# Wide predicated copies in a chunked linear recurrence, and a shorter weight look-ahead ahead of paired blocks

## The chip, the cores and the metric

The kernel runs on one core of a Trainium2 chip. Its engines each work through an instruction stream of their own: TensorE (PE) multiplies matrices, with weight loads (PEld) that overlap the products; VectorE (DVE), ScalarE (ACT) and GpSimd (POOL) compute elementwise; SyncE (SP) issues most transfers. The metric is the device time of one execution in microseconds (us). Before the change it is 2135.25 us, the median of three runs (2132.23 to 2136.88).

## The reference, cut to what matters

Two layers (DEPTH 2) work on 512 frames of width 1024, in float32. Each layer has a half-step SwiGLU feed-forward block (inner width 2816), a token mixer, a cross-attention into 256 memory tokens and a second feed-forward block:

```python
def swiglu(h, w1, w3, w2):
    return (jax.nn.silu(h @ w1) * (h @ w3)) @ w2

# mixer, head group A: 4 heads, key and value width 128
S_t = diag(f_t) S_{t-1} + k_t outer v_t      # k_t = 1 - f_t
o_t = S_t^T q_t
# head group B: trailing means over 2, 4, 8, 16 frames minus the frame, then a linear map
x = x + concat(o_a, o_b) @ w_out
```

The causal score of frame t against an earlier frame s inside a chunk is the sum over the key width of q_t, k_s and the product of all decays f between them. This part, and the feed-forward products, are what the change touches.

## The kernel before, in words

**Layout.** Activations lie with features on the 128 partitions and the 512 frames along the free axis. Each float32 operand is split into a high and a low part of the type that TensorE multiplies fast (`split`: a CAST on ACT, line 76, writes the high part `whi`, a subtraction on DVE, line 77, writes the low part `wlo`), and every product is three matmuls (`mm3`, lines 84 to 86: high by high, high by low, low by high). So nearly all of the time is in lines 84 to 86.

**Order of the work.** The program text sets an order, and a scheduler that simulates the engines places the instructions of each engine's stream; in a stream, everything runs in that fixed order, and an instruction that waits holds all behind it. Rings of tiles limit how far work runs ahead: one shared ring ("s") of 38 SBUF tiles holds weights as loaded (`raw`, `wsum`), weights split (`whi`, `wlo`), and mixer tiles such as `spread` and `packed`. A transfer into a ring tile waits until the tile's last reader is done.

**Weights.** `Weights` is a list of all weight pieces in order of use. A piece is a column tile (1024 by 128), a group of rows, or a *block*: two neighbouring column tiles of which a Strassen-like scheme (`Pairs`) forms sums. A block is loaded by four transfers on SP's queue (lines 130 to 133) and a fifth on POOL's queue that adds the second column tile onto the first in memory (line 134); it is then split in several steps (raw, the loaded sum, sums made on DVE in lines 163 and 164, and a quarter tile `w`). `next` is called when a piece is to be used: it finishes the splits under way, and then starts the splits of the pieces ahead. `ahead(i, n)` walks on from piece i until n units are passed, a block counting two. The split look-ahead is 4 units where the piece itself is a block and `SPLIT` = 5 elsewhere; the load look-ahead is `LOAD` = 7. The feed-forward blocks use plain column tiles for the first 6 or 8 of 22 column tiles, then blocks, in three parts, each followed by its rows of w2. So the list passes from plain pieces to blocks 11 times in the program.

In `Pairs.block` a product's result stays in PSUM until ACT has copied it (`keep`, line 545) or DVE has added it; between products, `wts.step()` takes the next split step. `xall` (line 436) adds the finished rows of w2 to the residual on DVE.

**The mixer's levels.** Scores inside a chunk of 128 frames are built by doubling: at level m = 1, 2, 4, ... 64, frames pair up in runs of 2m, the second half of a run against the first half. `atd` holds the scores of two heads (one *pair of heads* g) over four chunks. For m from 2 to 16, `dense` lets TensorE multiply the packed first halves (`keys`) with the second halves of `qf` (line 768), ACT copies the PSUM result to `packed` (line 777), and transfers on ACT's queue (line 782) spread its rows over the partitions where they belong, into the tile `spread`, which was set to zero once. `place` then copies, under a mask, from `spread` into `atd` (line 740; for m = 1 straight from PSUM): one copy of 128 partitions by 64 elements per head and chunk. At m = 32, `dense` copies small tiles from PSUM (line 773); at m = 64 TensorE multiplies directly (line 815) and DVE copies (line 816). After each level, `kg` and `qf` are multiplied by the decay of the run (`tot`; lines 822 and 824, one operation per head) and `tot` by itself (line 827). The copies of level m/2 stand in the program behind the first pair's decays of level m.

`levels` is a generator that is stepped between other work of the mixer: the value projection (`v`, line 906), the pooling head group (`u` line 917, POOL's additions into `sa` and `sb` line 920, `pt` lines 924 to 926), and weight splits. Behind the levels, `states` transposes `kg` (line 847, copied to `kt` by ACT) and multiplies it with `v` (line 856).

Of the kernel before, what the change touches and what calls it, by code (L numbers as in the profile page):

```python
# [7 lines left out]
F32 = mybir.dt.float32  # L8
# [3 lines left out]
ALU = mybir.AluOpType  # L12
AX = mybir.AxisListType

P = 128
D = 1024
T = 512
# [3 lines left out]
NT = T // P  # L21
# [25 lines left out]
def trunk_kernel(ctx: ExitStack, tc: tile.TileContext, ap: dict, out: bass.AP):  # L47
    nc = tc.nc
    pe, act, dve, pool = nc.tensor, nc.scalar, nc.vector, nc.gpsimd
# [11 lines left out]
    def ps_tile():  # L61
        return pp.tile([P, 512], F32, tag="ps", name="ps")
# [5 lines left out]
    def s_tile(shape, dt, name):  # L68
        return sp.tile(shape, dt, tag="s", name=name)
# [19 lines left out]
    class Weights:  # L89
# [107 lines left out]
        def next(self):  # L197
            i = self.at
            self.at += 1
            while self.todo:  # L200
                self.step()
            block = len(self.src[i]) == 2
            ahead = [*self.ahead(i, 4 if block else self.SPLIT)]
            if i + 3 == len(self.src) - 1:
                ahead.append(i + 3)
            for j in ahead:
                if j not in self.hl:
                    self.todo.append(self.cut(j))
                    if not block or j == i:
                        while self.todo:  # L210
                            self.step()
            for j in self.ahead(i, self.LOAD):
                self.load(j)
            return self.hl.pop(i)
# [53 lines left out]
    masks = {}  # L268
# [421 lines left out]
    def mix(l, norm, mem, after):  # L690
        f = [s_tile([P, 2, T], F32, "f") for _ in range(2)]
        kg = [s_tile([P, 2, T], F32, "kg") for _ in range(2)]
        q = [s_tile([P, 2, T], F32, "q") for _ in range(2)]
        qf = [s_tile([P, 2, T], F32, "qf") for _ in range(2)]
        atd = [s_tile([P, 2, NT, P], F32, "atd") for _ in range(2)]
# [24 lines left out]
        def products(a, b):  # L720

            t = tp.tile([P, T], F32, tag="sq", name="qk", bufs=4)
            hl = s_tile([P, 2, T], F32R, "qkp")
            pool.tensor_tensor(t if len(a.shape) == 2 else t.rearrange("p (h n) -> p h n", h=2), a, b, op=ALU.mult)
            split(hl[:, 0], hl[:, 1], t)
            return hl

        def column_sums(ps, hl):

            for c in range(2):  # L730
                pe.matmul(ps, ones_r, hl[:, c], start=c == 0, stop=c == 1)

        def place(g, m, rows):

            for hh in range(2):
                o = atd[g][:, hh].rearrange("p i (b e j) -> p i b e j", e=2, j=m)
                src = rows[:, hh * 256:(hh + 1) * 256].rearrange("p (i b j) -> p i b j", i=NT, j=m)
                mk = masks[m].rearrange("p (b j) -> p b j", j=m)
                for i in range(NT):
                    dve.copy_predicated(o[:, i, :, 1, :], mk, src[:, i])  # L740

        keys = [None, None]

        def first_halves(g, m):


            keys[g] = tp.tile([P, T], F32, tag="sq", name="keys", bufs=4)
            src = kg[g].rearrange("p h (b e j) -> p h b e j", e=2, j=m)[:, :, :, 0, :]
            if m > 4:
                act.copy(keys[g].rearrange("p (h b j) -> p h b j", h=2, j=m), src)  # L750
                return
            for hh in range(2):
                dst = keys[g][:, hh * HT:(hh + 1) * HT].rearrange("p (i j b) -> p i b j", i=NT, j=m)
                act.copy(dst, src[:, hh].rearrange("p (i b) j -> p i b j", i=NT))

        spread = s_tile([P, 2, T], F32, "spread")
        pool.memset(spread, 0.0)
        packed = [None]

        def dense(g, m):  # L760


            ps = ps_tile()
            for hh in range(2):
                for i in range(NT):
                    c = hh * HT + i * 64
                    b = qf[g][:, hh, i * P:(i + 1) * P].rearrange("p (b e j) -> p b e j", e=2, j=m)[:, :, 1, :]
                    pe.matmul(ps[0:64, c:c + 64], keys[g][:, c:c + 64], b, start=True, stop=True)
            if m == 32:
                for b in range(2):  # L770
                    src = ps[b * 32:b * 32 + 32].rearrange("p (h i t) -> p h i t", h=2, i=NT)[:, :, :, b * 32:b * 32 + 32]
                    for hh in range(2):
                        dve.tensor_copy(atd[g][b * 64:b * 64 + 32, hh, :, b * 64 + 32:b * 64 + 64], src[:, hh])  # L773
                return
            if g == 0:
                packed[0] = s_tile([64, 2, T], F32, "packed")
            act.copy(packed[0][:, g], ps[0:64])
            if g == 1:
                n = max(m, 64 // m)
                for x in range(64 // n):  # L780
                    rows = slice(x, P, 2 * m) if m <= 4 else slice(2 * m * x, 2 * m * x + m)
                    nc.scalar.dma_start(spread[rows], packed[0][x * n:(x + 1) * n])

        def levels():

            tot = f
            odd = [qf[g].rearrange("p h (n e) -> p h n e", e=2)[:, :, :, 1] for g in range(2)]
            even = [kg[g].rearrange("p h (n e) -> p h n e", e=2)[:, :, :, 0] for g in range(2)]  # L790
            near = [[products(q[g][:, hh], kg[g][:, hh]) for hh in range(2)] + [products(odd[g], even[g])] for g in range(2)]
            yield
            for m in (1, 2, 4, 8, 16, 32, 64):
                nb = T // (2 * m)
                tots = [None, None]
                for g in range(2):
                    if m == 1:
                        for hh in range(2):
                            ps = ps_tile()
                            column_sums(ps, near[g][hh])  # L800
                            dve.tensor_tensor(atd[g][:, hh], ps.rearrange("p (i t) -> p i t", t=P),
                                              ident.rearrange("p (o t) -> p o t", o=1).broadcast_to([P, NT, P]), op=ALU.mult)
                            yield
                        ps = ps_tile()
                        column_sums(ps, near[g][2])
                        place(g, m, ps)
                    elif m <= 32:
                        dense(g, m)
                    else:
                        ps = ps_tile()  # L810
                        for hh in range(2):
                            for i in range(NT):
                                a = kg[g][:, hh, i * P:i * P + 64]
                                b = qf[g][:, hh, i * P + 64:(i + 1) * P]
                                pe.matmul(ps[0:64, (hh * NT + i) * 64:(hh * NT + i + 1) * 64], a, b, start=True, stop=True)
                        dve.tensor_copy(atd[g][0:64, :, :, 64:128].rearrange("p h i t -> p (h i) t"),
                                        ps[0:64, :].rearrange("p (x t) -> p x t", t=64))
                    tv = tot[g].rearrange("p h (b e) -> p h b e", e=2)
                    kv = kg[g].rearrange("p h (b e j) -> p h b e j", e=2, j=m)
                    qv = qf[g].rearrange("p h (b e j) -> p h b e j", e=2, j=m)  # L820
                    for hh in range(2):
                        dve.tensor_tensor(kv[:, hh, :, 0, :], kv[:, hh, :, 0, :],
                                          tv[:, hh, :, 1:2].broadcast_to([P, nb, m]), op=ALU.mult)
                        dve.tensor_tensor(qv[:, hh, :, 1, :], qv[:, hh, :, 1, :],
                                          tv[:, hh, :, 0:1].broadcast_to([P, nb, m]), op=ALU.mult)
                    nt_ = s_tile([P, 2, nb], F32, "tot") if m == 1 else sm.tile([P, 2, nb], F32, tag=f"tot{m}", name="tot", bufs=2)
                    dve.tensor_tensor(nt_, tv[:, :, :, 0], tv[:, :, :, 1], op=ALU.mult)
                    tots[g] = nt_
                    if m < 32:
                        first_halves(g, 2 * m)  # L830
                    if g == 0 and 2 < m <= 32:
                        place(0, m // 2, spread[:, 0])
                        place(1, m // 2, spread[:, 1])
                    yield
                tot = tots
            last.extend(tot)
# [73 lines left out]
        for g in POOL_ORDER:  # L910
# [7 lines left out]
            src, dst, w_ = u, sa, 1  # L918
            while w_ < win:
                pool.tensor_tensor(dst[:, 16:], src[:, 16:], src[:, 16 - w_:16 + T - w_], op=ALU.add)  # L920
                src, dst = dst, (sb if dst is sa else sa)
# [16 lines left out]
        o = [None] * H  # L938
# [296 lines left out]
```

## Time and profile before

| | |
|---|---|
| median of 3 runs | 2135.25 us (2132.23 to 2136.88) |
| profiled execution | 2134.99 us, span from first to last instruction 2133.2 us |
| mean granted TensorE clock | 0.994 |
| instructions in the trace | 31051 |
| PE busy | 2106.7 us (99%) |
| DVE busy | 1370.6 us (64%) |
| ACT busy | 901.2 us (42%) |
| POOL busy | 225.5 us (11%) |
| read from HBM | 259.85 MB |

Busy time is the union of an engine's instructions. Successive matmuls overlap in the records, so their rate is read from start to start: 0.227 us for 512 columns, 0.120 us for 256 at full clock. In a timeline, a row gives start, duration, engine, line, operation and tiles (output, then inputs), the count of like instructions in a row, and in brackets the idle time of the engine ahead of it with what ended it. A wait that names an engine and a line is one for that engine's result, or for a tile that it frees.

### The profile page before, as it was taken

The numbers are of one execution on the slowest core, as the hardware profiler recorded it, in microseconds if no ns is written. First come the engines' busy times: TensorE is split into PE (matmuls) and PEld (weight loads), VectorE is DVE, ScalarE is ACT, GpSimd is POOL, SyncE is SP. The second block draws the span as 40 slices with busy tenths as digits, with TensorE's granted clock in tenths as the row PEclk, the third lists the DMA queues.
The fourth block names the chain that finished last, engine by engine and source line by source line (L and its number), as shares of the span: only waits on it lengthen the run. The fifth ranks groups of instructions, "written<-read, shape, count | busy, mean of one in ns | idle before, by whom it ended". The sixth has DMA issues, their size and how long they took to land. (4 is left out here: it accounts for less than half of the span.)

```text
span 2133.2 us, 31051 instructions
## 1 busy us (share of the span) xinstructions
PE 2106.7 (99%) x12380; PEld 1858.4 (87%) x12380; DVE 1370.6 (64%) x2104; ACT 901.2 (42%) x1397; POOL 225.5 (11%) x216
## 2 busy tenths in 40 slices
PE   9999999999999999999999999999999999999998
PEld 7889898887988888999988998988789888889896
DVE  6747565687646485755676575658875556657565
ACT  4425345433534343544444353434244443435254
POOL 1100000312000020000011000003110001100002
PEclk9999999999999999999999999999999999999999
DMA  4355465222424245737325745532334331475453
GB/s 176 107 158 149 119 170 167 68 86 95 143 79 138 62 113 144 190 104 193 127 57 151 193 119 164 167 104 73 86 110 133 109 104 50 140 202 133 135 154 117
DMA packets 106866, 271.58 MB, mean 127 GB/s; under 512 B 10592, under 2 KB 10592, under 8 KB 106720
## 3 DMA queue, kind: packets, MB, share of 16 engines
q1 hardware_dynamic: 92944, 227.85, 32.0%
q0 software_dynamic: 11952, 38.02, 10.2%
q10 hardware_dynamic: 1824, 3.73, 0.8%
q8 instruction: 97, 1.59, 0.3%
q14 instruction: 49, 0.40, 0.1%
HBM read 259.85 MB, written 2.10 MB: 123 GB/s over the span
## 5 line engine op out<-in xcount | busy, mean ns | idle before, releaser
L77 DVE TENSOR_TENSOR wlo<-raw,whi 128x1024 fp32r<-128x1024 f32 (+1 forms) x329 | 404.5, 1250 | 81.2 <-ACT whi L76 73.7
L76 ACT CAST whi<-raw 128x1024 fp32r<-128x1024 f32 (+1 forms) x329 | 335.0, 1046 | 118.3 <-DMA raw<-in_ffn_w_dram 57.3
L84 PE MATMUL ps<-h,whi 128*128 128x512 f32 x848 | 333.4, 395 | 5.1 <-DVE atd L773 4.1
L85 PE MATMUL ps<-h,whi 128*128 128x512 f32 x848 | 333.3, 393 | 0.5 <-DVE h L80 0.5
L86 PE MATMUL ps<-h,wlo 128*128 128x512 f32 x848 | 332.0, 392 | 0.4 <-DVE wlo L77 0.4
L84 PE MATMUL ps<-bh,whi 128*128 128x256 f32 x744 | 210.1, 284 | 3.4 <-ACT keep L545 2.8
L84 PE MATMUL acc<-bh,whi 128*128 128x256 f32 x744 | 211.1, 284 | 1.9 <-ACT keep L545 1.9
L85 PE MATMUL acc<-bl,whi 128*128 128x256 f32 x744 | 211.0, 284 | 0.0
L86 PE MATMUL acc<-bh,wlo 128*128 128x256 f32 x744 | 210.9, 284 | 0.0
L86 PE MATMUL ps<-bh,wlo 128*128 128x256 f32 x744 | 210.9, 283 | 0.0
L85 PE MATMUL ps<-bl,whi 128*128 128x256 f32 x744 | 210.8, 283 | 0.0
L77 DVE TENSOR_TENSOR wlo<-wsum,whi 128x1024 fp32r<-128x1024 f32 x124 | 154.9, 1249 | 69.3 <-ACT whi L76 68.1
L76 ACT CAST whi<-wsum 128x1024 fp32r<-128x1024 f32 x124 | 130.1, 1050 | 157.9 <-DVE wsum L164 85.5
L84 PEld LDWEIGHTS ps<-h,whi 128*128 128x128 f32 x848 | 160.9, 190 | 40.0 <-issue 4.3
L85 PEld LDWEIGHTS ps<-h,whi 128*128 128x128 f32 x848 | 160.9, 190 | 35.7 <-DVE h L80 2.5
L86 PEld LDWEIGHTS ps<-h,wlo 128*128 128x128 f32 x848 | 160.8, 190 | 34.5 <-DVE wlo L77 0.8
L84 PEld LDWEIGHTS ps<-bh,whi 128*128 128x128 f32 x744 | 142.6, 192 | 4.3 <-ACT keep L545 3.1
L84 PEld LDWEIGHTS acc<-bh,whi 128*128 128x128 f32 x744 | 143.2, 192 | 2.6 <-ACT keep L545 2.3
L85 PEld LDWEIGHTS acc<-bl,whi 128*128 128x128 f32 x744 | 143.3, 193 | 0.3
L85 PEld LDWEIGHTS ps<-bl,whi 128*128 128x128 f32 x744 | 143.0, 192 | 0.6
L86 PEld LDWEIGHTS acc<-bh,wlo 128*128 128x128 f32 x744 | 143.3, 193 | 0.0
L86 PEld LDWEIGHTS ps<-bh,wlo 128*128 128x128 f32 x744 | 143.0, 192 | 0.0
(262 smaller groups left out, 4295.4 us busy)
## 6 DMA issues: line engine op xcount, KB each, us to landing
raw<-in_ffn_w_dram SPq DMA_DIRECT2D x207, 512.0 KB
wsum<-in_ffn_w_dram SPq DMA_DIRECT2D x124, 256.0 KB
wsum<-in_ffn_w_dram POOLq DMA_DIRECT2D x62, 512.0 KB, 6.3
raw<-in_ffn_w_dram SPq DMA_DIRECT2D x64, 256.0 KB
raw<-in_w_in_dram SPq DMA_DIRECT2D x32, 512.0 KB
raw<-in_w_out_dram SPq DMA_DIRECT2D x16, 512.0 KB
raw<-in_xa_wk_dram SPq DMA_DIRECT2D x16, 512.0 KB
raw<-in_xa_wq_dram SPq DMA_DIRECT2D x16, 512.0 KB
```

What stands on the lines that cost most here:

```text
L76: act.copy(hi, src)
L77: dve.tensor_tensor(lo, src, hi.bitcast(F32), op=ALU.subtract)
L84: pe.matmul(o, a[0], b[0], start=start, stop=False, skip_group_check=more)
L85: pe.matmul(o, a[0], b[1], start=False, stop=False, skip_group_check=more)
L86: pe.matmul(o, a[1], b[0], start=False, stop=stop, skip_group_check=more)
```

## The change

Four things change; the arithmetic stays the same.

1. `place` issues one predicated copy per pair of heads, over both heads and four chunks (128 x 512), where it issued eight of 128 x 64. Sixteen copies of a level become two, 160 of the program become 20.
2. The decays of `kg` and `qf` are multiplied over both heads in one operation (128 x 512) instead of two (128 x 256): 112 operations become 56.
3. There are two `spread` tiles, used in turn by the levels 2, 4, 8 and 16, and one more memset on POOL in each layer. Both copies of a level now stand behind the second pair's decays of the next level instead of the first pair's.
4. In `Weights.next`, the split look-ahead is 4 units instead of 5 as soon as one of the next four pieces is a block, and not only where the piece itself is one. The loads' look-ahead stays at 7.

```diff
             block = len(self.src[i]) == 2
-            ahead = [*self.ahead(i, 4 if block else self.SPLIT)]
+            near = any(len(x) == 2 for x in self.src[i:i + 4])
+            ahead = [*self.ahead(i, 4 if near else self.SPLIT)]
...
         def place(g, m, rows):
-            for hh in range(2):
-                o = atd[g][:, hh].rearrange("p i (b e j) -> p i b e j", e=2, j=m)
-                src = rows[:, hh * 256:(hh + 1) * 256].rearrange("p (i b j) -> p i b j", i=NT, j=m)
-                mk = masks[m].rearrange("p (b j) -> p b j", j=m)
-                for i in range(NT):
-                    dve.copy_predicated(o[:, i, :, 1, :], mk, src[:, i])
+            o = atd[g].rearrange("p h i (b e j) -> p (h i) b e j", e=2, j=m)[:, :, :, 1, :]
+            src = rows.rearrange("p (x b j) -> p x b j", x=2 * NT, j=m)
+            mk = masks[m].rearrange("p (o b j) -> p o b j", o=1, j=m).broadcast_to([P, 2 * NT, 64 // m, m])
+            dve.copy_predicated(o, mk, src)
...
-        spread = s_tile([P, 2, T], F32, "spread")
-        pool.memset(spread, 0.0)
+        spreads = [s_tile([P, 2, T], F32, "spread") for _ in range(2)]
+        for t in spreads:
+            pool.memset(t, 0.0)
+        spread = {m: spreads[i % 2] for i, m in enumerate((2, 4, 8, 16))}
...
-                    nc.scalar.dma_start(spread[rows], packed[0][x * n:(x + 1) * n])
+                    nc.scalar.dma_start(spread[m][rows], packed[0][x * n:(x + 1) * n])
...
-                    for hh in range(2):
-                        dve.tensor_tensor(kv[:, hh, :, 0, :], kv[:, hh, :, 0, :],
-                                          tv[:, hh, :, 1:2].broadcast_to([P, nb, m]), op=ALU.mult)
-                        dve.tensor_tensor(qv[:, hh, :, 1, :], qv[:, hh, :, 1, :],
-                                          tv[:, hh, :, 0:1].broadcast_to([P, nb, m]), op=ALU.mult)
+                    kv = kg[g].rearrange("p h (b e j) -> p (h b) e j", e=2, j=m)
+                    qv = qf[g].rearrange("p h (b e j) -> p (h b) e j", e=2, j=m)
+                    tx = tot[g].rearrange("p h (b e) -> p (h b) e", e=2)
+                    dve.tensor_tensor(kv[:, :, 0, :], kv[:, :, 0, :], tx[:, :, 1:2].broadcast_to([P, 2 * nb, m]), op=ALU.mult)
+                    dve.tensor_tensor(qv[:, :, 1, :], qv[:, :, 1, :], tx[:, :, 0:1].broadcast_to([P, 2 * nb, m]), op=ALU.mult)
...
-                    if g == 0 and 2 < m <= 32:
-                        place(0, m // 2, spread[:, 0])
-                        place(1, m // 2, spread[:, 1])
+                    if g == 1 and 2 < m <= 32:
+                        for x in range(2):
+                            place(x, m // 2, spread[m // 2][:, x])
```

The scheduler's order moves with this. Three places matter below. Rows give the line, the operation, output and inputs, and the access pattern; lines of the changed kernel are one off those before (L739 is `place`, L774 the small copies of m = 32, L817 the copies of m = 64, L546 `keep`, L923 to L925 `pt`).

First, DVE at the end of layer 0's levels, from the copies of level 16 on, before:

```order
L740 COPY_PREDICATED atd<-fixed,spread 128x4x16 x5
L773 COPY atd<-ps 32x4x32 x4
L824 TENSOR_TENSOR qf<-qf,tot 128x8x32
L740 COPY_PREDICATED atd<-fixed,spread 128x4x16 x3
L824 TENSOR_TENSOR qf<-qf,tot 128x8x32
L77 TENSOR_TENSOR wlo<-raw,whi 128x1024
L773 COPY atd<-ps 32x4x32
L824 TENSOR_TENSOR qf<-qf,tot 128x8x32
L740 COPY_PREDICATED atd<-fixed,spread 128x4x16 x8
L773 COPY atd<-ps 32x4x32 x2
L924 SCALAR_TENSOR_TENSOR pt<-sa,u 128x512
L773 COPY atd<-ps 32x4x32
```

and with the change:

```order
L77 TENSOR_TENSOR wlo<-raw,whi 128x1024
L774 COPY atd<-ps 32x4x32 x4
L824 TENSOR_TENSOR qf<-qf,tot 128x16x32
L774 COPY atd<-ps 32x4x32 x4
L824 TENSOR_TENSOR qf<-qf,tot 128x16x32
L739 COPY_PREDICATED atd<-fixed,spread 128x32x16 x2
L923 SCALAR_TENSOR_TENSOR pt<-sa,u 128x512
L77 TENSOR_TENSOR wlo<-raw,whi 128x1024
L924 TENSOR_TENSOR pt<-sa,fixed 128x8
L916 TENSOR_TENSOR u<-ps,rrow 128x512
L925 TENSOR_TENSOR pt<-pt,u 128x8
L817 COPY atd<-ps 64x8x64
```

The small copies from PSUM and the last decays of `qf` now stand ahead of the level-16 copies, which were spread among them.

Second, ACT where layer 0's second feed-forward block passes from column tiles to blocks, before:

```order
L76 CAST whi<-raw 128x1024
L545 COPY keep<-ps 128x256
L76 CAST whi<-wsum 128x1024
L545 COPY keep<-acc 128x256
L545 COPY keep<-ps 128x256
```

and with the change:

```order
L76 CAST whi<-raw 128x1024
L546 COPY keep<-ps 128x256
L546 COPY keep<-acc 128x256
L76 CAST whi<-wsum 128x1024
L546 COPY keep<-ps 128x256
```

The second `keep` has moved ahead of the CAST of a loaded sum.

Third, SP's queue at layer 0's first feed-forward block, where its second part begins: the last load of the second block and the first ones of the third, with the engines and queues whose semaphores they wait for, before:

```order
L133 DMA raw_984<-in_ffn1_w3_dram 128x512 [waits DMAHW7_49]
L130 DMA wsum_1056<-in_ffn1_w1_dram 128x512 [waits DMAHW0_49,DMAHW6_49,DVE_49,Activation_49]
L131 DMA wsum_1056<-in_ffn1_w1_dram 128x512 [waits DMAHW1_49]
L132 DMA raw_1057<-in_ffn1_w1_dram 128x1024 [waits DMAHW2_49,PE_49]
L133 DMA raw_1058<-in_ffn1_w1_dram 128x512 [waits DMAHW3_49,PE_49]
```

and with the change:

```order
L133 DMA raw_984<-in_ffn1_w3_dram 128x512 [waits DMAHW7_49]
L130 DMA wsum_1038<-in_ffn1_w1_dram 128x512 [waits DMAHW0_49,DVE_49]
L131 DMA wsum_1038<-in_ffn1_w1_dram 128x512 [waits DMAHW1_49]
L132 DMA raw_1039<-in_ffn1_w1_dram 128x1024 [waits DMAHW3_49,DMAHW2_49,DVE_49]
L133 DMA raw_1040<-in_ffn1_w1_dram 128x512 [waits PE_49]
```

The order of the transfers is the same, but the third block's tile is an earlier one of the ring, and its first load no longer waits for ACT and the second block's transfers (the DVE instruction that it waits for is an earlier one as well).

More of the change, by code (lines that the diff above doesn't have):

```diff
@@ L818, in levels @@
                     tv = tot[g].rearrange("p h (b e) -> p h b e", e=2)
-                    kv = kg[g].rearrange("p h (b e j) -> p h b e j", e=2, j=m)
-                    qv = qf[g].rearrange("p h (b e j) -> p h b e j", e=2, j=m)
-                    for hh in range(2):
-                        dve.tensor_tensor(kv[:, hh, :, 0, :], kv[:, hh, :, 0, :],
-                                          tv[:, hh, :, 1:2].broadcast_to([P, nb, m]), op=ALU.mult)
-                        dve.tensor_tensor(qv[:, hh, :, 1, :], qv[:, hh, :, 1, :],
-                                          tv[:, hh, :, 0:1].broadcast_to([P, nb, m]), op=ALU.mult)
+                    kv = kg[g].rearrange("p h (b e j) -> p (h b) e j", e=2, j=m)
[3 more added lines that the diff above has]
+                    dve.tensor_tensor(qv[:, :, 1, :], qv[:, :, 1, :], tx[:, :, 0:1].broadcast_to([P, 2 * nb, m]), op=ALU.mult)
                     nt_ = s_tile([P, 2, nb], F32, "tot") if m == 1 else sm.tile([P, 2, nb], F32, tag=f"tot{m}", name="tot", bufs=2)
```

## The prediction

> **What bounds the kernel now.** I read the page first, then the waits of TensorE, then the timelines around each of those waits.
>
> ```profile
> PE 2106.7 (99%) x12380; PEld 1858.4 (87%) x12380; DVE 1370.6 (64%) x2104; ACT 901.2 (42%) x1397; POOL 225.5 (11%) x216
> ```
>
> TensorE is busy for 99% of the span and the change takes no matmul away. DVE has a third of the span free, so a microsecond saved on DVE is worth nothing by itself. What can be won is time in which TensorE waits, and time in which it runs at half clock. The waits of TensorE, with total, count and longest:
>
> ```profile
> PE ps L84 <- DVE atd L773: 4.1, 2, 2.0
> PE ps L815 <- DVE qf L824: 3.2, 3, 1.1
> PE ps L84 <- ACT keep L545: 2.8, 1, 2.8
> PE acc L84 <- ACT keep L545: 1.9, 2, 1.0
> PE ps L84 <- DVE xall L436: 0.5, 1, 0.5
> ```
>
> The first two rows (7.3 us) lie in the `levels` of the two layers, where predicated copies and decays run. The other three (5.2 us) lie where the feed-forward weights go over from other work to paired column blocks, where the rule in `Weights.next` decides. The waits left out here have to do with neither.
>
> Behind the longer of these waits the matmuls start further apart for a while. Layer 0 (start, duration, instruction, wait before it):
>
> ```profile
> 494.06 0.77 PE L84 MATMUL ps<-h,whi 128*128 128x512 f32 x1 [2.04 <-DVE atd L773]
> 494.62 0.63 PE L85 MATMUL ps<-h,whi 128*128 128x512 f32 x1
> ...
> 499.74 0.44 PE L85 MATMUL ps<-h,whi 128*128 128x512 f32 x1
> ...
> 500.25 0.39 PE L84 MATMUL ps<-h,whi 128*128 128x512 f32 x1
> 500.48 0.39 PE L85 MATMUL ps<-h,whi 128*128 128x512 f32 x1
> ```
>
> There are 13 starts from 494.06 to 499.74, in 5.68 us; at the later interval of 0.23 they take 2.99, so 2.7 us are lost to the clock after a wait of 2.0. Windows give the same for the other two places (columns: window, length, busy time and count of each engine, granted clock, DMA share, GB/s):
>
> ```profile
> 150.00:165.00 15.00, 12.15 (x89) 11.95 (x88) 6.16 (x9) 4.60 (x10) 1.72 (x2) 0.89 0.95 250
> 495.00:502.00 7.00, 7.00 (x22) 5.52 (x21) 6.74 (x16) 0.00 (x0) 2.49 (x4) 0.66 0.00 0
> 1541.00:1550.00 9.00, 5.97 (x25) 4.85 (x26) 8.83 (x25) 1.05 (x1) 2.49 (x4) 0.81 0.06 20
> ```
>
> 0.11 of 15 us is 1.65 us in the feed-forward of layer 0. 0.19 of 9 us is 1.7 us in layer 1, part of it idle time anyway; I take 1.5.
>
> So the rows have the half clock behind waits of 2.04 and 2.85 us, and I count it as a cost of those waits. The Trainium skill (TensorE: Matmul & The Clock Gate, Part 1) puts it after at least one idle window of about 3.4 us. By that rule none of these waits would be enough alone. That the lost clock does not come back with the waits is a rival below.
>
> **Levels: copies and decays.** The copies of one layer from the spread tile (16 more come from PSUM at level 1):
>
> ```profile
> L740 DVE COPY_PREDICATED atd<-fixed,spread 128x64 f32<-128x64 int32 x64 | 13.1, 306 | 5.1 <-DMA spread<-packed 5.1
> ```
>
> Durations overlap, so the price is the interval from start to start, from the timeline of DVE:
>
> ```profile
> 457.64 2.27 DVE L740 COPY_PREDICATED atd<-fixed,spread 128x64 f32<-128x64 int32 x16 [1.87 <-DMA spread<-packed]
> 459.81 0.75 DVE L824 TENSOR_TENSOR qf<-qf,tot 128x256 f32<-128x256 f32 x2
> 476.24 4.20 DVE L740 COPY_PREDICATED atd<-fixed,spread 128x64 f32<-128x64 int32 x16 [1.08 <-DMA spread<-packed]
> 480.35 0.41 DVE L824 TENSOR_TENSOR qf<-qf,tot 128x256 f32<-128x256 f32 x1
> 480.69 1.21 DVE L77 TENSOR_TENSOR wlo<-raw,whi 128x1024 fp32r<-128x1024 f32 x1
> 481.82 0.68 DVE L924 SCALAR_TENSOR_TENSOR pt<-sb,u 128x512 f32<-128x512 f32 x1
> ```
>
> Sixteen copies take 2.17 us from 457.64 to 459.81, 0.136 each. A decay of 256 elements takes 0.34 (480.35 to 480.69), the tensor operation of 1024 takes 1.13 (480.69 to 481.82), so a line through both gives 0.60 for 512 elements (the row at 481.82 lasts 0.68, with the part that overlaps its successor). No row shows a predicated copy of 512. It costs at least 8 × 64 elements at that slope, 0.54, and at most what the eight small ones cost now, 1.09, unless the wide pattern is slower than the narrow one, which nothing bears out. I take 0.60. Ten wide copies then replace 80 in a layer: 80 × 0.136 − 10 × 0.60 = 4.9 us of DVE (0 at the other bound). The decays: 28 operations of 512 replace 56 of 256, 28 × (2 × 0.34 − 0.60) = 2.2 us. One more memset on the idle POOL is nothing on the path.
>
> The row at 476.24 is 2 us longer than its like. POOL was adding then:
>
> ```profile
> 476.29 1.07 POOL L920 TENSOR_TENSOR sa<-sb 128x512 f32<-128x512 f32 x1
> 477.44 1.28 POOL L920 TENSOR_TENSOR sb<-sa 128x512 f32<-128x512 f32 x1
> ```
>
> Each of the two additions holds DVE for about 1 us. If fewer DVE instructions met fewer holds, up to 2 us more would be won here; I leave both holds in, since a wide copy runs as long as four small ones and is as likely to be caught. The Trainium skill (GPSIMD Engine Reference, 1. Specifications) has POOL's SBUF interface shared with VectorE, with contention for DVE instructions with two SBUF inputs; by it the holds stay, without it the sum would be 2 us larger at most.
>
> Two tiles in turn remove a wait on ACT's queue. Now the transfers of level 16 stand behind the copies of level 8 (DVE done at 480.4), with their source ready at 474.84 (ACT, then DVE):
>
> ```profile
> 474.27 0.57 ACT L777 COPY packed<-ps 64x512 f32<-64x512 f32 x1
> 480.51 2.46 ACTq L782 DMA_DIRECT2D spread<-packed  x4
> 483.01 1.05 ACT L76 CAST whi<-raw 128x1024 fp32r<-128x1024 f32 x1 [8.16 <-DMA spread<-packed]
> ...
> 484.96 2.47 DVE L740 COPY_PREDICATED atd<-fixed,spread 128x64 f32<-128x64 int32 x5 [1.24 <-DMA spread<-packed]
> 487.34 0.97 DVE L773 COPY atd<-ps 32x128 f32<-32x128 f32 x4
> ```
>
> Four triggers and the landing take 4.45 us (480.51 to 484.96); from 474.9 they end at 479.3, before DVE gets there. The CAST goes 5 us earlier too. DVE's time line then: the level-8 copies at 476.24 take 1.2 plus the two holds, done at 479.3 instead of 480.35. Up to the second qf of level 32 follow a qf of 0.6, two wlo (2.3), pt, u and pt (1.5), eight L773 copies at some 0.22 (1.8; four stand in the last row) and two qf (1.2): the first qf ends at 485.2 (TensorE needs it at 487.13), the second at 486.7. Before, TensorE waited for them here:
>
> ```profile
> 487.13 0.68 PE L815 MATMUL ps<-qf,kg 128*64 128x64 f32 x8
> 488.82 1.42 PE L815 MATMUL ps<-qf,kg 128*64 128x64 f32 x16 [1.02 <-DVE qf L824]
> 491.34 0.68 PE L815 MATMUL ps<-qf,kg 128*64 128x64 f32 x8 [1.10 <-DVE qf L824]
> ...
> 502.30 0.81 PE L847 MATMUL ps<-fixed,kg 128*128 128x128 f32 x6
> ```
>
> If POOL's later additions land on this chain, each adds 1 us, and two would eat the margin. The L773 copies, which free the bank behind the 2.04 wait, are no longer last. So 1.02 + 1.10 + 2.04 + 2.7 = 6.9 us are to be had in layer 0, and 1.10 + 2.04 + 1.5 = 4.6 in layer 1. What is late next is kg of level 64, which the transposes of L847 need at 502.30 before, 495.4 with all 6.9 us gone. From 486.7 DVE has two copies (1.2), pt and wlo (1.8), u (0.7), L816 and kg twice (2.4): 492.8, or 494.8 with two holds. Thin but enough; I deduct 1.5 us in each layer for holds and small waits: **5.4 + 3.1**.
>
> **Weights.** At the feed-forward transition of layer 0:
>
> ```profile
> 126.69 1.23 DVE L77 TENSOR_TENSOR wlo<-wsum,whi 128x1024 fp32r<-128x1024 f32 x1 [1.17 <-ACT whi L76]
> 129.07 0.43 SPq L133 DMA_DIRECT2D raw<-in_ffn_w_dram  x1
> ...
> 142.38 0.33 SPq L130 DMA_DIRECT2D wsum<-in_ffn_w_dram  x1
> 147.14 0.86 POOL L134 DMA_DIRECT2D wsum<-in_ffn_w_dram  x1 [14.08 <-DVE xall L436]
> 156.34 1.04 ACT L76 CAST whi<-wsum 128x1024 fp32r<-128x1024 f32 x1 [5.96 <-issue]
> 157.70 0.39 PE L84 MATMUL ps<-bh,whi 128*128 128x256 f32 x1 [2.85 <-ACT keep L545]
> ```
>
> The third block's first load goes out at 142.38, its adding transfer at 147.14, and ACT's CAST of the sum starts at 156.34, 9.2 us later, with the keep copies behind it, and TensorE waits for keep. The new order cuts the second block later, so the tile that the third block's load takes is one freed by DVE at 127.9 (the first row) rather than at 142.3: SP issues right behind the second block's last load, about 129.5. With the same 14 us to landing it is there at 143.5 to 148, ahead of its use. That removes 2.85 + 1.65. The xall copies are now spread between the second block's preparations, which takes the 0.52 as well; I deduct 0.7 because the second block's adding transfer now shares its time with the third block's loads. **4.3**.
>
> At the two passages from columns to blocks one keep copy stands behind such a CAST; in the new order it stands ahead of it:
>
> ```profile
> 793.80 1.05 ACT L76 CAST whi<-wsum 128x1024 fp32r<-128x1024 f32 x1 [4.11 <-issue]
> 794.75 0.37 ACT L545 COPY keep<-acc 128x256 f32<-128x256 f32 x1
> ```
>
> That removes 1.03 and 0.86: **1.9**. The other eight transitions have no wait now.
>
> **Sum.** 5.4 + 3.1 + 4.3 + 1.9 = 14.7 us from the profiled 2134.99, which is 0.26 under the median of the runs: 2120.5.
>
> **Rivals.**
>
> *Half of it arrives.* Either the levels keep their waits, because the holds by POOL and the later place of the copies (behind the second pair, not the first) use up what DVE saved, or the weights do. Then 6.2 or 8.5 us are won: 2126 to 2129. For it: the margins of 0.4 to 2 us above are each within two holds. Against: a whole load wait and 4.9 us of copies leave the chain.
>
> *Nothing measurable changes.* If a wide copy costs 1.09 and the waits move to kg of level 64, levels give about 2, with new clock loss nothing, and the weights 2: 2131 to 2135.
>
> *The half clock stays.* If it follows a window of idle time and not the one wait, or has a cause of its own, the 2.7 and 1.5 us of the levels stay as they are: 14.7 − 4.2 = 10.5 us won, 2124.7. For it: waits of 1.02 and 1.10 us stand close ahead of the 2.04. Against: TensorE waits for nothing else there. By the page's window of 3.4 us it would be so if short waits remain that add up.
>
> *Second block late, slower.* Preparing less ahead puts the second block's adding transfer (SP and POOL queues) in one stretch with the third's loads. Its last piece is ready just where TensorE needs it; 4 us late costs 4 + 1.65 by the clock. There are 11 such transitions, eight with no wait now. With the levels' 8.5 kept and 6.2 lost, the kernel is slower from two such new waits on: 2 × 5.65 = 11.3 against 8.5, so 2138. Against it: the third block's loads fall into a stretch in which SP issued nothing (129.5 to 142.38), and only one step of the look-ahead is lost.
>
> **Chances.** The forecast as told, 11 to 18 us won, 0.54; the half clock stays 0.07; half 0.16; nothing 0.14; slower 0.09. A measurement of this kernel tells about 0.2% (4.3 us) from no change, so the first three are faster: 0.77. The likeliest one's own range is 2116 to 2125. For 8 in 10 the range reaches from 2115, all of the 18.4 us to be had and some luck, to 2132.
>
> **What would show it.** Right: rows L815 and L773 gone from the waits of TensorE, the clock 1.00 in the windows behind, no keep row at 157, spread no longer what DVE waits for, predicated copies of 128x512 at an interval near 0.60. Wrong: a wait of TensorE of 2 us or more for kg (L847), or for xall or wlo at a transition, with half clock behind it; a wide copy above 1.1 us.

## The result and the profile after

The changed kernel takes 2119.08 us, the median of four runs (2117.84 to 2120.76), beside 2134.47 us of the kernel before on the same chip (2132.23 to 2136.88). The ratio is 0.9928, with a 95% interval of 0.9911 to 0.9945. Two later timings of the same kernel on other occasions gave 0.9940 (0.9926 to 0.9953) both times. By the medians the gain is 15.4 us here and 12.6 and 12.9 us in those two. The profiled execution (2120.76 us, the longest of the four) has a span of 2118.9 us, 14.3 us less than before.

The waits of TensorE after the change that have to do with it (total, count, longest):

```profile
PE ps L846 <- DVE u L916: 2.7, 2, 1.4
PE ps L84 <- ACT keep L546: 0.7, 1, 0.7
```

The rows for atd, qf and xall are gone, and of keep 0.7 us is left. One row is new: the transposes of the states (L846) wait for u, once in each layer. Where the time went is read from the starts of corresponding matmuls in both traces (they run in the same number, 12380):

| stretch | gained (us) | forecast |
|---|---|---|
| head, to 74 us | −0.39 | |
| feed-forward transition of layer 0 | 5.4 | 4.3 |
| layer 0's levels and states | 4.5 | 5.4 |
| passage at 795 us | 0.1 | 1.9 for both |
| passage at 1144 us | 1.1 | |
| layer 1's levels and states | 3.5 | 3.1 |
| sum | 14.2 | 14.7 |

At the feed-forward transition, SP and ACT now (SP's first row is the third block's first load):

```profile
129.99 0.38 SPq L130 DMA_DIRECT2D wsum<-in_ffn_w_dram  x1
...
149.11 0.36 ACT L546 COPY keep<-acc 128x256 f32<-128x256 f32 x1
149.37 1.05 ACT L76 CAST whi<-wsum 128x1024 fp32r<-128x1024 f32 x1
151.16 0.37 ACT L546 COPY keep<-ps 128x256 f32<-128x256 f32 x1 [0.74 <-PE ps L86]
```

The load goes out at 129.99 instead of 142.38, the sum is cast at 149.37 instead of 156.34, and keep waits for TensorE, not TensorE for keep.

At the end of layer 0's levels DVE reads like this; the three instructions of 1.5 us are what the forecast called holds:

```profile
478.82 0.69 DVE L824 TENSOR_TENSOR qf<-qf,tot 128x512 f32<-128x512 f32 x1
...
480.55 1.53 DVE L824 TENSOR_TENSOR qf<-qf,tot 128x512 f32<-128x512 f32 x1
482.00 1.35 DVE L739 COPY_PREDICATED atd<-fixed,spread 128x512 f32<-128x512 int32 x2
...
486.44 1.54 DVE L823 TENSOR_TENSOR kg<-kg,tot 128x512 f32<-128x512 f32 x1
487.91 1.52 DVE L824 TENSOR_TENSOR qf<-qf,tot 128x512 f32<-128x512 f32 x1
...
492.14 0.68 DVE L916 TENSOR_TENSOR u<-ps,rrow 128x512 f32<-128x512 f32 x1
```

TensorE runs its level-64 products without a break and then waits where u has to free a bank of PSUM:

```profile
481.94 2.08 PE L816 MATMUL ps<-qf,kg 128*64 128x64 f32 x32
...
492.88 0.55 PE L846 MATMUL ps<-fixed,kg 128*128 128x128 f32 x3 [1.36 <-DVE u L916]
```

The last qf of level 32 is ready at 482.08. TensorE, which arrives at 481.94, finds it just in time. The forecast had 486.7 and 487.13, on a clock that reads 5.2 us later.

### The profile page after: what moved, and what is told of

Read it like the earlier page. It is cut to its first block, busy times and chain, and to the rows that moved or that the text cites. A ratio compares the mean times of both kernels' runs of the same rounds, so it can differ in the third digit from the quotient of the medians.

```text
span 2118.9 us, 30843 instructions
## 1 busy us (share of the span) xinstructions
PE 2101.4 (99%) x12380; PEld 1854.5 (88%) x12380; DVE 1353.5 (64%) x1908; ACT 901.4 (43%) x1397; POOL 234.2 (11%) x218
```

## The experiments

Two theories stood against each other at first: that the parts add up, each in its own stage (A), and that one part does the work and another does nothing (B, C, D by the part). From the first traces a third question came: why the half clock came and went.

### Each half alone

```diff
 weights_only: the kernel before, and
+            near = any(len(x) == 2 for x in self.src[i:i + 4])
+            ahead = [*self.ahead(i, 4 if near else self.SPLIT)]

 levels_only: the changed kernel, and
-            ahead = [*self.ahead(i, 4 if near else self.SPLIT)]
+            ahead = [*self.ahead(i, 4 if block else self.SPLIT)]
```

> The kernel before with the new look-ahead rule alone; copies, decays and spread tile as before. Theory A (the parts add up, each in its own stage): the keep waits at 157, 795 and 1144 us go or shrink, with the half clock at 158 to 162, some 6.5 us; the waits on atd (two of 2.0) and qf (1.0 to 1.1) in the levels stay: 2128 us, ratio 0.997. Rival B (the wide copies give everything, the rule only moves waits about): within 2 us of the kernel before, 2133 to 2136.

> The changed kernel with the old look-ahead rule; wide copies, wide decays and two spread tiles stay. Theory A: the waits on keep of 2.85 and 1.9 us are there again, the waits on atd and qf in the levels stay away, the new waits of 1.4 us of the transposes for u are there: some 8.5 us gained, 2126 us, ratio 0.996. Rival B (wide copies give everything): 2119 to 2120.

Measured: the rule alone 2127.76 us, ratio 0.9968 (0.9955 to 0.9981); the levels alone 2123.82 us, ratio 0.9949 (0.9934 to 0.9963). The sum of the two gains is 0.83% beside 0.72% and 0.60% in the timings of the whole: the parts add up within the intervals. Theory A held in time for the rule (2128 expected); the levels gave 2 us more than expected (2126). Waits of TensorE, with the rule alone and with the levels alone:

```profile
PE ps L84 <- DVE atd L774: 4.1, 2, 2.0
PE ps L816 <- DVE qf L825: 3.3, 3, 1.1
...
PE ps L84 <- ACT keep L546: 0.4, 1, 0.4
```

```profile
PE ps L84 <- ACT keep L545: 2.9, 1, 2.9
PE ps L845 <- DVE u L915: 2.7, 2, 1.4
...
PE acc L84 <- ACT keep L545: 1.0, 1, 1.0
```

The rule alone leaves the waits of the levels as they were. The levels alone bring back the wait of 2.9 us for keep and the one at the passage of 1144 us (1.0 us), but not the 0.5 us for xall and not the wait at 795 us, which the forecast gave to the rule. And behind the 2.9 us no half clock stands this time, which is worth 1.65 us and is taken up below. Together these three are some 3 us of this trace, which covers the 2 us beyond what was expected. At 795 us the starts of the matmuls show 1.3 us gained by the rule alone, 1.2 by the levels alone and 0.1 by both together, so there the parts do not add up; why is told further down.

### The second tile

```diff
 one_spread_tile: the changed kernel, and
-        spreads = [s_tile([P, 2, T], F32, "spread") for _ in range(2)]
+        spreads = [s_tile([P, 2, T], F32, "spread")]
 one_tile_early_copies: the same, and
-                    if g == 1 and 2 < m <= 32:
+                    if g == 0 and 2 < m <= 32:
```

> The changed kernel with one spread tile for all levels again. Theory A (my prediction's step: the second tile takes 5 us of waiting off the transfers of level 16): the transfers of a level wait for the copies of the level before, DVE is 3 us or more later at the last decays of qf, and TensorE waits 1 to 3 us for qf in each layer, with half clock behind the longer ones: 2122 to 2126. Rival C (the width of the copies is what pays, the tile nothing): 2119, no wait for qf.

> The changed kernel with one spread tile and the copies of a level behind the first pair's decays of the next level, as before the change, so that the transfers of a level stand behind the copies of the level before. Theory A: the transfers of level 16 start 1 to 4 us later than with two tiles, DVE waits for them, and TensorE waits 0.5 to 3 us in each layer for u or qf beyond now: 2120 to 2124 beside 2119. Rival C (the tile is worth nothing): equal to the changed kernel within 1 us.

The first of the two does not do what it was meant to: with one tile and the copies behind the second pair, a level's copies stand behind the next level's transfers into the same tile, so they take the next level's rows and also wait for its transfers. It took 2126.72 us, and its waits for qf (5.1 us) come from that; it tells nothing of the tile.

The second keeps the order right and took 2123.68 us (2122.84 to 2123.72) beside 2118.55 us (2117.76 to 2120.11) of the changed kernel on the same chip. ACT and DVE in it:

```profile
469.10 0.58 ACT L778 COPY packed<-ps 64x512 f32<-64x512 f32 x1
473.25 2.46 ACTq L783 DMA_DIRECT2D spread<-packed  x4
```

```profile
479.26 0.75 DVE L739 COPY_PREDICATED atd<-fixed,spread 128x512 f32<-128x512 int32 x1 [2.26 <-DMA spread<-packed]
```

and the wait of TensorE that follows:

```profile
PE ps L816 <- DVE qf L824: 3.9, 3, 1.6
```

The transfers of level 16 start at 473.25, behind the copies of level 8, where the changed kernel has them at 469.81; DVE waits 2.26 us for them, and the waits for qf are back. So the tile with the later place of the copies that it permits is worth some 5 us, part of it half clock: this run's profile has 6.8 us of half clock from 485 us on. The two were not tried apart.

### The width of copies and decays

```diff
 narrow_copies: the changed kernel with the loop of place before
-            dve.copy_predicated(o, mk, src)
+            for hh in range(2):
...
+                for i in range(NT):
+                    dve.copy_predicated(o[:, i, :, 1, :], mk, src[:, i])
 narrow_decays: the changed kernel with
+                    for hh in range(2):
+                        dve.tensor_tensor(kv[:, hh, :, 0, :], kv[:, hh, :, 0, :],
+                                          tv[:, hh, :, 1:2].broadcast_to([P, nb, m]), op=ALU.mult)
...
```

> The changed kernel with eight copies of 128x64 in place of each wide one, at the same places of the program. Theory A: each level costs DVE 0.9 to 1.0 us more (16 times 0.136 against two of 0.62), so the last qf comes 1 to 2 us later than now (it now ends just when TensorE arrives), and the transposes' wait for u grows from 1.4 to 2.5 or more: 2121 to 2125. Rival D (the new order of the copies of level 32 ahead of those of level 16, not their width, took the waits away): 2119 to 2120.

> The changed kernel with eight copies of 128x64 for each wide one, beside the unaltered one. Its first trace had waits of 3.4 (transposes for u) and 2.5 us (products with kt for atd) where the changed kernel had 2.7 and none. Theory A (width pays through DVE's chain at the end of the levels): 3 us from these waits and up to 3 us of half clock more, 2122 to 2125 beside 2119. Rival D (the first timing was the chip's): equal within 1 us.

> The changed kernel with the decays by head again, two of 256 elements for one of 512. By the intervals of before (0.34 against 0.60) each costs DVE 0.08 us more, 2.2 us in a layer of which 0.6 us lie behind the copies of level 8. Theory A: the wait of the transposes for u grows by some 0.5 us in each layer, 2119 to 2122 beside 2119. Rival: the shorter pieces meet POOL's additions with one short instruction and nothing changes.

Narrow copies took 2124.99 us, and in the second timing 2124.19 us (2123.07 to 2126.77) beside 2120.03 us (2118.56 to 2120.81) of the changed kernel on the same chip, timed once more there:

> The changed kernel unaltered, beside the narrow copies on the same chip: 2119 us. By theory E its two waits of 1.4 to 1.6 us of the transposes bring half clock in either, both or neither layer, whichever way they fall on the grid of 3.41 us.

The width of the copies is worth some 4 us, with half clock in it. Narrow decays took 2120.96 us (2119.67 to 2122.38) beside 2118.55 us (2117.76 to 2120.11); the ranges overlap, so 2.4 us is a likely value and no more. Its trace points the same way: TensorE waits 4.4 us at the states of the two layers, where the changed kernel waits 2.7 to 3.0. Waits of TensorE with narrow copies:

```profile
PE ps L848 <- DVE u L918: 3.4, 2, 1.7
PE ps L857 <- DVE atd L819: 2.5, 2, 1.3
```

The waits for qf do not come back, as theory A had expected them to: by then the order of the last levels suffices (rival D is right on that point). What the longer copies cost shows later, in 5.9 us of waits at the states where the changed kernel has 2.7 to 3.0.

### What the wait for u is made of

The changed kernel's remaining wait has two possible makers: DVE's chain behind level 32, two operations of which last 1.5 us, or the bank and ACT's kt copies themselves. First, the last decay of qf goes from DVE to ACT, which is idle there:

```diff
 last_decay_on_act
-                    dve.tensor_tensor(qv[:, :, 1, :], qv[:, :, 1, :], tx[:, :, 0:1].broadcast_to([P, 2 * nb, m]), op=ALU.mult)
+                    if m < 64:
+                        dve.tensor_tensor(qv[:, :, 1, :], qv[:, :, 1, :], tx[:, :, 0:1].broadcast_to([P, 2 * nb, m]), op=ALU.mult)
+                    else:
+                        for hh in range(2):
+                            for b in range(nb):
+                                half = qf[g][:, hh, b * P + 64:(b + 1) * P]
+                                act.activation(half, half, AF.Copy, scale=tot[g][:, hh, 2 * b:2 * b + 1])
```

> The changed kernel with the last decay of qf (level 64) on ACT, as 16 scaled copies of 64 elements in each layer, in place of two operations of DVE. Theory G (the transposes' wait of 1.4 us for u is DVE's chain behind the last levels, two operations of which POOL's additions hold to 1.5 us): u comes 1.2 to 2.1 us earlier, the wait is gone or under 0.3 us in both layers, 2.7 us less and no half clock in the levels: 2115 to 2117 beside 2119. Rival H (the wait is set by PSUM's bank or by ACT's copies kt, not by DVE's chain): the wait stays, or moves to kt behind ACT's 16 copies, and the time with it: 2119 to 2121.

Measured: 2114.39 us (2114.17 to 2115.35) beside 2118.55 us of the changed kernel (2117.76 to 2120.11); against the kernel before 0.9921 (0.9907 to 0.9934). DVE and ACT of it:

```profile
486.04 1.54 DVE L823 TENSOR_TENSOR kg<-kg,tot 128x512 f32<-128x512 f32 x1
...
489.94 0.68 DVE L922 TENSOR_TENSOR u<-ps,rrow 128x512 f32<-128x512 f32 x1
```

```profile
482.12 3.93 ACT L830 ACTIVATE qf<-qf,tot 128x64 f32<-128x64 f32 x16
489.64 0.86 ACT L854 COPY kt<-ps 128x384 f32<-128x384 f32 x2 [3.60 <-PE ps L852]
```

From the start of kg's decay to u it is 3.9 us instead of 5.7, the transposes no longer wait, and ACT's 16 copies are done 3.6 us before the first transposes give it work again. Theory G held, with 0.6 us beyond the range that it expected, and this version beats both kernels.

Second, what makes the operations of 1.5 us:

```diff
 no_pool_additions
-                pool.tensor_tensor(dst[:, 16:], src[:, 16:], src[:, 16 - w_:16 + T - w_], op=ALU.add)
+                pool.tensor_copy(dst[:, 16:], src[:, 16:])
```

> The changed kernel with each two-input addition of the pooling group on POOL replaced by a one-input copy of the same size: the trailing means are left out, all else runs. Theory J (POOL's two-input additions hold DVE's two-input operations): the decays of 1.5 us at the end of the levels last 0.67 to 0.7 us, no copy or decay lasts over 1.0 us but those of levels 1 and 2, u comes 1.5 us or more earlier and the transposes' wait goes: 2114 to 2117. Rival K (any work of POOL, or the transfers at that time, slow DVE): decays of 1.5 us stay.

One execution took 2115.58 us. DVE and POOL at the end of layer 0's levels:

```profile
484.24 0.67 DVE L823 TENSOR_TENSOR kg<-kg,tot 128x512 f32<-128x512 f32 x1
...
485.44 1.21 DVE L77 TENSOR_TENSOR wlo<-raw,whi 128x1024 fp32r<-128x1024 f32 x1
```

```profile
485.16 2.47 POOL L919 COPY sb<-sa 128x512 f32<-128x512 f32 x1
```

The decays last 0.67 and 0.68 us, and the transposes do not wait. These two run for the most part beside an idle POOL; the row that meets a copy of POOL is the wlo at 485.44. It takes its usual 1.2 us, and the copy on POOL takes 2.47 where one takes 0.61 alone. In the changed kernel a wlo that met an addition lasted 2.06 us (at 471.70). So theory J held for the decays, and rival K in part: other work of DVE is still stretched beside the one-input copies, by up to 0.4 us (a decay of 0.92 at 487.25, a pt of 1.09, a wlo of 1.63 at 471.51), where an addition costs up to 0.87. Nor does an addition always win: the one that starts at 476.77 in the changed kernel, behind a wlo of DVE that is under way, takes 2.04 us itself and the wlo its usual 1.22. The Trainium skill (GPSIMD Engine Reference, 1. Specifications) has POOL's SBUF interface shared with VectorE and contended by DVE instructions with two SBUF inputs; the rows agree, and add that it matters how many inputs POOL's own instruction has.

### The price of a wide copy

The forecast took 0.60 us for each wide copy. From start to start, those of levels 4, 8 and 16 take 0.60 to 0.62 us where nothing holds them; but those of level 1, from PSUM, and of level 2, from SBUF, take 1.10 to 1.17. The first row here is level 2, the second level 4:

```profile
443.75 2.50 DVE L739 COPY_PREDICATED atd<-fixed,spread 128x512 f32<-128x512 int32 x2 [2.99 <-DMA spread<-packed]
...
452.51 1.32 DVE L739 COPY_PREDICATED atd<-fixed,spread 128x512 f32<-128x512 int32 x2 [1.68 <-DMA spread<-packed]
```

```diff
 runs_of_16
         def place(g, m, rows):
+            m = 16
```

> The changed kernel with the access pattern of level 16 (runs of 16 elements) in the copies of all levels: the scores land in wrong places, as many elements are copied. In the changed kernel copies of levels 4, 8 and 16 start 0.60 to 0.62 us apart, those of level 1 (from PSUM) and level 2 (from SBUF) 1.13 to 1.17. Theory L (runs of one or two elements cost 2 ns an element): all copies 0.60 to 0.65, level 1 from PSUM too. Rival M (PSUM as source costs it at level 1, something else at level 2): level 1 stays at 1.13.

The copies from PSUM of the changed kernel and of this run (duration in ns, least, median, largest):

```profile
L739 DVE COPY_PREDICATED atd<-fixed,ps x4: 1317/1340/1343, 423.0 to 1475.6; 128x512 f32<-128x512 int32 x4
```

```profile
L740 DVE COPY_PREDICATED atd<-fixed,ps x4: 722/740/755, 422.9 to 1472.7; 128x512 f32<-128x512 int32 x4
```

In runs of 16, level 1 lasts 0.74 us and level 2 starts 0.61 to 0.64 us apart. Theory L held: the source is not what costs. The narrow copies of before fit this. Eight of level 1 took 1.10 us (the next instruction started at 429.83), as much as one wide copy of that level now:

```profile
428.73 1.31 DVE L740 COPY_PREDICATED atd<-fixed,ps 128x64 f32<-128x64 int32 x8
```

At levels 1 and 2 the width therefore saves nothing; at the other three it saves 0.48 us a copy. Whether the runs of the mask, of the source or of the target make the difference was not tried.

### The half clock

> The changed kernel once more, unaltered, to stand beside the others on the same chip and to show the spread of one kernel. The waits of TensorE should be those of the first trace (the transposes for u 1.4 us in each layer, keep 0.7 us): 2119 us. Theory E (the half clock comes when a window of 3.41 us of a grid that runs free of the kernel holds TensorE busy for half of its time or less): the same waits, but half clock behind them in other places than before, 0 to 3 stretches of 3.4 us between 100 and 2100 us. Rival F (a wait of a given length always has it): half clock at 493 us again and none in layer 1.

The three traces of the same changed kernel have the same wait for u in each layer (1.35 to 1.6 us). The first has half clock behind it in layer 0 alone, the second in layer 1 alone, the third in neither. Windows of the first trace, cut where its clock changes (0.50 and 1.00 are the granted clock), and the same of the second:

```profile
489.90:493.31 3.41, 1.81 (x15) 1.38 (x13) 2.86 (x7) 1.12 (x3) 0.40 (x1) 1.00 0.01 2
493.31:496.72 3.41, 3.41 (x11) 2.20 (x10) 2.15 (x6) 1.43 (x3) 0.64 (x1) 0.50 0.87 305
1537.80:1541.21 3.41, 2.16 (x12) 1.63 (x13) 2.19 (x8) 1.45 (x4) 1.04 (x1) 1.00 0.45 136
1541.21:1544.62 3.41, 3.41 (x17) 2.13 (x16) 2.74 (x7) 2.23 (x5) 0.00 (x0) 1.00 0.77 278
```

```profile
489.44:492.85 3.41, 1.81 (x15) 1.38 (x13) 2.86 (x7) 1.13 (x3) 0.41 (x1) 1.00 0.01 2
492.85:496.27 3.42, 3.42 (x18) 1.98 (x16) 2.72 (x9) 2.29 (x5) 0.63 (x1) 1.00 0.93 303
1534.10:1537.51 3.41, 1.56 (x11) 1.29 (x11) 2.75 (x7) 0.92 (x3) 0.52 (x1) 1.00 0.03 5
1537.51:1540.92 3.41, 3.41 (x10) 1.99 (x9) 2.34 (x7) 1.43 (x3) 0.52 (x1) 0.50 0.85 302
```

In the third trace the windows behind both waits have the full clock:

```profile
492.50:496.00 3.50, 3.23 (x17) 2.03 (x17) 2.35 (x8) 1.66 (x4) 1.04 (x1) 1.00 0.76 263
1538.50:1542.00 3.50, 3.50 (x18) 2.06 (x16) 2.71 (x9) 2.28 (x5) 0.72 (x1) 1.00 0.86 299
```

And the kernel before, at its three places between head and tail:

```profile
155.06:158.47 3.41, 0.77 (x6) 0.77 (x7) 1.06 (x1) 1.59 (x3) 0.00 (x0) 1.00 1.07 318
158.47:161.89 3.42, 3.42 (x18) 3.42 (x18) 2.12 (x5) 2.02 (x4) 0.86 (x1) 0.50 0.68 201
489.57:492.98 3.41, 1.35 (x16) 1.07 (x16) 3.33 (x14) 1.04 (x1) 0.00 (x0) 1.00 0.06 23
492.98:499.81 6.83, 5.75 (x14) 4.53 (x15) 6.74 (x13) 0.00 (x0) 2.49 (x4) 0.50 0.00 0
1540.87:1544.29 3.42, 0.70 (x9) 0.54 (x8) 3.31 (x15) 1.05 (x1) 0.00 (x0) 1.00 0.16 63
1544.29:1547.70 3.41, 2.99 (x7) 2.44 (x8) 3.35 (x6) 0.00 (x0) 1.19 (x2) 0.50 0.02 5
```

Every stretch of half clock ahead of the tail lasts 3.41 or 6.83 us, and the beginnings lie on a grid: 492.98 − 158.47 = 334.51 is 98.0 times 3.4133, and 1544.29 − 492.98 = 1051.31 is 308.0 times. The grid lies elsewhere from trace to trace. Behind a window in which TensorE was busy for 0.70, 0.77, 1.35 or 1.56 us, the next is at half clock; behind one of 1.81 us it is so in one trace and not in the other; behind one of 2.16 it is not. Rival F is refuted, and theory E held in this form: not the length of a wait decides, but how much of it falls into one window. Its bound of half a window is not exact. In the traces of all runs windows busy for 1.61 to 1.82 us went either way, and in the first 20 us nine traces have half clock behind windows in which TensorE was busy for 1.9 to 2.35 us, so the busy time is not the whole of it. The wait of 2.9 us for keep with the levels alone fits: it falls on two windows, busy for 2.27 and 1.61 us, and neither has half clock behind it. The second lies where either is seen, so there it may be luck:

```profile
151.98:155.40 3.42, 2.27 (x19) 2.06 (x18) 0.00 (x0) 0.00 (x0) 0.86 (x1) 1.00 1.04 287
155.40:158.81 3.41, 1.61 (x13) 1.61 (x14) 1.91 (x3) 1.90 (x4) 0.00 (x0) 1.00 1.08 302
158.81:162.22 3.41, 3.41 (x31) 3.41 (x30) 2.81 (x5) 2.23 (x5) 0.86 (x1) 1.00 0.48 123
```

The Trainium skill (TensorE: Matmul & The Clock Gate, Part 1) gives the window as 3413 ns and calls it free-running; these traces agree with both. Its condition, an idle window, is too strict for this case: a window that was busy for 1.35 us was enough.

## Why the prediction was right

**Time.** 2120.5 us was forecast, 2119.08 us was measured, within the likeliest case's own range of 2116 to 2125, and faster. In the profiled executions 14.7 us were forecast and 14.3 us are found. The mechanism was right stage by stage. That the sum is so close is partly luck: the stages are off by +1.1, −0.7, −0.9 and +0.4 us, which nearly cancel, and a half clock of 1.7 us that the first trace has and the third has not could have moved it either way.

**Weights, FFN transition (4.3 forecast, 5.4 found).** The chain came as described: tile freed earlier, load at 129.99 (forecast 129.5), cast ahead of its use, no wait for keep or xall. The deduction of 0.7 us for the shared time of the second block's adding transfer was not needed: it does land later, 8.5 us behind its issue instead of 6.4, but TensorE does not wait for it. The rival of a late second block did not happen at any of the 11 transitions: no new wait for whi or wlo stands in the list.

**Weights, the two passages (1.9 forecast, 1.2 found).** At 1144 us it came as forecast (1.1 for 0.86). At 795 us the step "in the new order it stands ahead of it" counted only one of the keep copies. The next one, which still stands behind the CAST of the loaded sum, is now the one that TensorE waits for:

```profile
786.21 1.05 ACT L76 CAST whi<-wsum 128x1024 fp32r<-128x1024 f32 x1 [4.65 <-DMA wsum<-in_ffn_w_dram]
787.16 0.37 ACT L546 COPY keep<-ps 128x256 f32<-128x256 f32 x1
```

```profile
787.58 0.39 PE L84 MATMUL ps<-bh,whi 128*128 128x256 f32 x1 [0.68 <-ACT keep L546]
```

The CAST waits for the adding transfer of its block, and that varies from trace to trace. With the new order it landed 7.3 us behind its issue (the rule alone), 8.1, 8.9 and 9.1 (the three traces of the changed kernel), and TensorE waited 0, 0.24, 0.68 and 0.67 us. With the old order it took 6.6 (the kernel before) and 5.7 (the levels alone), and TensorE waited 1.03 and 0 us. So the new order stands a later transfer, as the forecast had it, but the transfer is as much a part of this wait, and the forecast had no term for it. Why its time varies stays open.

**Levels (5.4 + 3.1 forecast, 4.5 + 3.5 found).** The waits for atd and qf went entirely. The 1.5 us set aside in each layer "for holds and small waits" became one wait of 1.36 us in each; not at kg of level 64, which was named as the next to be late, but one step behind it, at the bank that u frees at the end of the same chain of DVE. Layer 0 falls 0.9 us short; the half clock of 3.41 us behind that wait (1.7 us lost), which no term had, is more than that.

**The price of a wide copy.** 0.60 us was right for three levels of five. For levels 1 and 2 it was mis-sized: 1.10 to 1.17, at and a little above the upper bound of 1.09. The condition "unless the wide pattern is slower than the narrow one" was not the trouble; the bound was read from copies of level 4 alone, and a wide copy of level 1 costs what its eight narrow ones cost. (The lower bound comes out at 0.53 by its own slope, not 0.54.) DVE is saved some 2.9 us by the copies in a layer (6 copies that save 0.48 each), not 4.9. That seems to have cost nothing: those levels run long before TensorE waits, and with runs of 16 in all levels, which takes half a microsecond off each of these copies, TensorE still waited 3.0 us for u and the one execution took 2120.63 us.

**The half clock.** The step "I count it as a cost of those waits" is right on average and wrong as a rule: the 2.7, 1.65 and 1.5 us were what one execution happened to have. The rival "the half clock stays" was in part true of the profiled execution after, and false of the third trace.

**Second tile.** The forecast moved the transfers of level 16 up by 5.6 us (480.51 to 474.9). With wide copies in both, the run with one tile shows 3.4 us, and some 5 us of time that hang on it.

**Its own signs.** Three did not come as told. The clock behind the wait in layer 0 was not 1.00 in the first trace. DVE no longer waits for spread at level 16, but still does at the levels before (10.3 us in 5 waits of the whole program, 10.5 in 7 before); no wait of TensorE in the list hangs on them. And copies above 1.1 us, named as a sign of being wrong, are there at levels 1 and 2.

## What to carry to other kernels

Where the busiest engine is busy for 99%, list its waits, follow each to the chain that ends it, and ask which instruction of that chain will be last once the wait is gone: here it was u, a few instructions behind the kg that was named. Moving work to an engine that idles in that stretch (the last decay to ACT, 4.2 us by the medians) can be worth as much as making the work itself shorter. Two parts of a change can take the same wait away, as at 795 us, and then their gains do not add. A wait's price has a part that is drawn anew at each execution, so compare kernels by the waits in several traces and by timed medians, and not by one trace's clock.

## What the runs showed of the hardware that was not expected

- Between head and tail the half clock of TensorE comes in whole windows of 3.413 us, on a grid that lies elsewhere in each trace. The same wait of 1.35 to 1.6 us brought it in layer 0, in layer 1 or in neither.
- A predicated copy of 128x512 takes 0.60 to 0.62 us in runs of 4 elements or more and 1.10 to 1.17 us in runs of 1 or 2; from PSUM in runs of 16 it takes 0.62 to 0.64, much as from SBUF. Eight copies of 128x64 take 1.08 to 1.15 us in either case.
- A two-input addition of 512 elements on POOL holds a two-input operation of DVE that starts behind it for 0.9 us (1.54 for 0.67); behind a wlo under way it is held itself (2.04 us for 1.04). With a one-input copy on POOL it is mostly POOL that waits (2.47 us for 0.61), and DVE lost 0.4 us at most.
